# Block addresses, the order of loads at a stage turn, and the weight sums of the down projection in a one-core encoder layer

## The chip, the cores and the metric

The kernel runs on one core of a Trainium2 chip. The metric is the device time of one execution in microseconds (us). A core has a matrix engine (TensorE, PE in the profile, with PEld for its weight loads), a vector engine (VectorE, DVE), an activation engine (ScalarE, ACT), GpSimd (POOL), and SyncE (SP), which here issues nearly all DMA transfers. SBUF is the on-chip memory of 128 partitions, PSUM the accumulators that PE writes.

## The reference

One layer of a streaming encoder is applied to 512 prompt frames and 64 sample frames, all float32. The core of it is:

```python
hn = rmsnorm(x, g_norm1)
proj = hn @ w_in                                   # 2048 -> 6144
q, k, v, gb, gc, hc = split(proj)
o_attn = stick_breaking(q, k, v)                   # 8 heads x 128
o_conv = gb * conv3_causal(gc * hc)                # 1024 channels
x = x + concat(rmsnorm(o_attn), rmsnorm(o_conv)) @ w_out
h2 = rmsnorm(x, g_norm2)
x = x + (silu(h2 @ w_gate) * (h2 @ w_up)) @ w_down # 2048 -> 5632 -> 2048
```

The new keys, values and convolution state are outputs too.

## The kernel before, in words

The 576 frames are processed together, in two halves of 288 (`HALF`), so nearly every matmul has 288 moving columns of 128 partitions. Activations lie transposed: channels on partitions, frames along the free dimension. Float32 accuracy is reached by splitting each operand into a high part (rounded to float32r) and the rest: a product is three matmuls, high weight with high frames, low with high, high with low (`step`, `multiply`). The split is one ACT copy and one DVE subtraction (`split`, L211 and L212).

The kernel has five stages, in order of time. The start loads and transposes x. Then come the input projection with attention and convolution woven into it (`head`, `conv_group`, L203), the output projection (`out_proj`, L203), the gate and up projections, and the down projection. Gate, up and down use a one-level Strassen scheme of seven products (L1117): a unit is a block of a weight matrix, 256 rows times m pairs by 256 columns, and its products carry the numbers 1 to 7. Each product is m x 3 matmuls. Gate and up units have m = 8. `DOWN` lists the down units as (column block, first pair, last pair), so m is the difference; there are 8 column blocks and 22 pairs of hidden rows, each pair being seven operand forms in DRAM (`hid_dram`, 2,016 KB). Seven slots in SBUF hold pairs for the down stage; they lie in blocks that the gate and up stage uses until its last unit (`h2s`, `t12`, `t34`), so the pairs can only be loaded when the last products that read these blocks are done. This place is the turn.

Weights come from DRAM into two raw tiles, `raw_a` and `raw_b`, each with two halves of 2,048 values per partition. A down unit with m up to 4 takes one half (`room`), a larger one both halves of one tile. `prepare(n, p)` runs four products ahead (`AHEAD`): it forms the weight operand of product p of unit n and splits it into `whl`, of which there are four. Four sums of weight blocks are needed per unit (L1085 to L1087 and L1099, all DVE). In the gate and up units the first three stand ahead of product 6 and the last ahead of product 3. In the down units the first three stand together behind the operand of product 2. When both products 3 and 4 of a unit have been prepared, its raw halves are free and `load_columns` issues the next loads that find room.

`run(n, p)` issues the matmuls and what follows them: after products 1, 6 and 5 the partial sum in PSUM is copied out by ACT (`kept`, L1127), and later products go on adding into the same PSUM tile, so PE waits for that copy. DVE and POOL add the results into accumulators in SBUF. The last unit of a column block calls `store_y`: PE transposes the accumulator (L1268), DVE copies two 128x128 blocks out of PSUM (L1270), ACT the remaining 32 rows (L1272), and SP stores. `load_pair` issues the load of a pair, L1247 as one DMA or L1239 as seven.

Until the last gate and up unit the scheduler orders all engines but PE. From the first product of that unit on (`NGU - 1`), ACT, DVE, SP and POOL go in the order written. `turned` says behind which product of the last unit which pairs may be loaded, and `since` and `PACE` spread the loads.

Pools are placed one behind the other from both ends of SBUF. In the built program `h2_s` begins at byte 72,416, `xhi` and `t12` at 155,616, the first `x2` tile at 192,480 and `mixa_hi` at 118,048 of the partition: the remainders by 128 are 96, 96, 96 and 32. The raw and split weight tiles begin at multiples of 128. Every half of 288 float32 values is 1,152 bytes, nine times 128.

Of the kernel before, what the change touches and what calls it, by code (L numbers as in the profile page):

```python
# [34 lines left out]
NP = KD // 2  # L35
# [6 lines left out]


DOWN = (
# [5 lines left out]
)  # L50


# [41 lines left out]
def tile_hybrid_stream_step(  # L94
# [6 lines left out]
    nc = tc.nc  # L101
# [12 lines left out]
    wpool = ctx.enter_context(tc.tile_pool(name="wpool", bufs=2, side="left"))  # L114
    rpool = ctx.enter_context(tc.tile_pool(name="rpool", bufs=1, side="left"))
    tmp = ctx.enter_context(tc.tile_pool(name="tmp", bufs=2, side="left"))
    acon = tc.alloc_tile_pool(name="acon", bufs=1, side="left")
    xt_dram = tc.dram_tile([KD, P, T], F32, name="xt_dram")
    x2_dram = tc.dram_tile([KD, P, T], F32, name="x2_dram")
# [90 lines left out]
    def split(hi, lo, src, lo_eng=None):  # L210
        nc.scalar.copy(out=hi, in_=src)  # L211
        (lo_eng or nc.vector).tensor_tensor(out=lo, in0=src, in1=hi.bitcast(F32), op=ALU.subtract)  # L212
# [796 lines left out]

    def load_columns(gone=()):  # L1010

        free.extend(gone)
        while wanted and room(*wanted[0]):
            n, c = wanted.pop(0)
            kind, i, a, m = UNITS[n]
            w = {"gate": w_gate, "up": w_up, "down": w_down}[kind]
            halves = room(n, c)
            for h in halves:
                free.remove(h)
            t = raw_tile[halves[0][0]]  # L1020
            t = t[:, halves[0][1], :] if len(halves) == 1 else t.rearrange("p h e -> p (h e)")
            wide_ = P if c is not None else 2 * P
            c0 = 2 * i * P + (c or 0) * P
            t = t[:, : 2 * m * wide_]
            nc.sync.dma_start(out=t.rearrange("p (k e) -> p k e", e=wide_),
                              in_=w[2 * a * P : 2 * (a + m) * P, c0 : c0 + wide_].rearrange("(k p) c -> p k c", p=P))
# [50 lines left out]
    unit = {}  # L1077
    operand = {}
    slot_turn = [0]

    def weight_sums(n, st):
        m = UNITS[n][3]
        st["a21"], st["a22"] = (region[n, 1][0][:, :, q, :] for q in range(2))
        st["s1"] = w2pool.tile([P, NP, P], F32, tag="s1", name="s1")[:, :m]
        nc.vector.tensor_tensor(out=st["s1"], in0=st["a21"], in1=st["a22"], op=ALU.add)  # L1085
        nc.vector.tensor_tensor(out=st["a21"], in0=st["a21"], in1=st["a11"], op=ALU.subtract)
        nc.vector.tensor_tensor(out=st["a11"], in0=st["s1"], in1=st["a11"], op=ALU.subtract)  # L1087

    def prepare(n, p_):

        st = unit.setdefault(n, {})
        m = UNITS[n][3]
        if p_ == 1:
            st["a11"], st["a12"] = (region[n, 0][0][:, :, q, :] for q in range(2))
        src = {1: "a11", 2: "a12", 3: "a12", 4: "a22", 5: "s1", 6: "a11", 7: "a21"}[p_]
        if p_ == 6 and n < NGU:
            weight_sums(n, st)
        if p_ == 3:
            nc.vector.tensor_tensor(out=st["a12"], in0=st["a12"], in1=st["a11"], op=ALU.subtract)  # L1099
        slot_turn[0] += 1  # L1100
        whl = wpool.tile([P, 2, NP, P], F32R, tag=("whi", "wlo")[slot_turn[0] % 2], name="whl")[:, :, :m]
        split(whl[:, 0], whl[:, 1], st[src])
        operand[n, p_] = whl
        if p_ == 2 and n >= NGU:
            weight_sums(n, st)
        if p_ in (3, 4):
            st["gone"] = st.get("gone", 0) + 1
            if n < NGU:
                load_columns(region.pop((n, p_ - 3))[1])
            elif st["gone"] == 2:  # L1110
                load_columns(region.pop((n, 0))[1])

    def multiply(ps, n, p_, start):
        whl, xs_ = operand.pop((n, p_)), frames(n, p_)
# [78 lines left out]
    for d, v in visits.items():  # L1193
        n = next(a for a, b in zip(v, v[1:]) if a >= NGU + 10 and b >= a + 4)
# [54 lines left out]
    def store_y(n, c, i):  # L1249

        d = UNITS[n][1]
        src, cs, f0 = acc[d, c, i], slice((2 * d + c) * P, (2 * d + c + 1) * P), HALVES[i][0]
        r = HALF - 2 * P

        def put(f, ap):

            rows, n_p = ap.shape[0], max(min(TP - f, ap.shape[0]), 0)
            if n_p:
                nc.sync.dma_start(out=yp[f : f + n_p, cs], in_=ap[:n_p])  # L1259
            if n_p < rows:  # L1260
                nc.sync.dma_start(out=ys[f + n_p - TP : f + rows - TP, cs], in_=ap[n_p:])  # L1261

        def work():
            yield 9
            po = misc("pot")[:, : 3 * P]
            for q in range(3):
                w = min(P, HALF - q * P)
                nc.tensor.transpose(po[:w, q * P : (q + 1) * P], src[:, q * P : q * P + w], ident)  # L1268
            ob = src[:, : 2 * P].rearrange("p (i c) -> p i c", c=P)
            nc.vector.tensor_copy(out=ob, in_=po[:, : 2 * P].rearrange("p (i c) -> p i c", c=P))  # L1270
            obs = down["pool"].tile([r, P], F32, tag="obs", name="obs", bufs=2)
            nc.scalar.copy(out=obs, in_=po[:r, 2 * P :])  # L1272
            yield 5
# [14 lines left out]
    pairs = []  # L1288
    since = PACE
    mode = ExitStack()  # L1290
    AHEAD = 4
    for k_ in range(AHEAD):
        prepare(*order[k_])
    for k_, (n, p_) in enumerate(order):
        if (n, p_) == (NGU - 1, 1):
            mode.enter_context(tc.manual_schedule(engines={mybir.EngineType.Activation, mybir.EngineType.DVE,
                                                           mybir.EngineType.SP, mybir.EngineType.Pool}))
# [4 lines left out]
        pairs += turned.get((n, p_), calls[n - NGU] if n >= NGU and p_ == 4 else ())  # L1302
        since += UNITS[n][3]
        if pairs and since >= (PACE if n >= NGU else NP if pairs[0] < 2 else 2 * NP):
            load_pair(pairs.pop(0))
            since = 0
        if p_ == 2:
            for d in residual.get(n, ()):
                add_residual(d)
# [39 lines left out]
```

## Time and profile before

| | us |
|---|---|
| median of 3 runs | 2469.44 (2468.92 to 2475.55) |
| the profiled execution | 2472.84 |
| its span, first to last instruction | 2471.1 |
| PE busy | 2426.1 |
| DVE busy | 1746.7 |
| ACT busy | 1076.7 |
| POOL busy | 236.5 |

The profile is of one execution. The span is 1.7 us shorter than that execution's own time. An engine counts as busy while any of its instructions runs. Matmuls overlap: each lasts about 297 ns from its start to its modelled end, and the next begins long before. The rate of PE is therefore read from the starts or from the number of matmuls in a stretch, not from the duration of one.

### The profile page before, as it was taken

To read this page: it belongs to the slowest core of one execution; us is meant where nothing else is said; L and a number is where in the kernel's file an instruction comes from. 1 tells how busy PE (TensorE), PEld (TensorE's weight loads), DVE (VectorE), ACT (ScalarE), POOL (GpSimd) and SP (SyncE) were. 2 spreads that over 40 slices of the span, in tenths; PEclk is the share of its full clock that TensorE was granted. 3 is DMA by queue.
4 is the path that set the end of the run, shared out by engine and by line. 5 is a ranking of instruction groups with operands and counts; after the bars stand their busy time and mean duration, and the time that the engine had idled before them with its cause. 6 is when DMAs were issued, how large, how long until landed. Compare 5 with 4: busy or idle time off the path is not lost. (4 is left out here: it accounts for less than half of the span.)

```text
span 2471.1 us, 44086 instructions
## 1 busy us (share of the span) xinstructions
PE 2426.1 (98%) x18137; PEld 2412.7 (98%) x18137; DVE 1746.7 (71%) x2686; ACT 1076.7 (44%) x1907; POOL 236.5 (10%) x340
## 2 busy tenths in 40 slices
PE   8999999999999999999999999999999899999997
PEld 8999999999999999999999999999999899999996
DVE  7766666363335457888888888888887678877776
ACT  5655555231122345444444444444444344434433
POOL 2111010110020120000000000000000103321221
PEclk9999999999999999999999999999999999999999
DMA  8232322232243333535444455344445928874632
GB/s 269 79 96 87 87 79 84 71 99 76 81 149 99 105 129 115 153 114 151 146 142 129 138 151 155 117 149 144 146 138 160 314 73 244 235 208 140 207 120 69
DMA packets 464547, 336.50 MB, mean 136 GB/s; under 512 B 10207, under 2 KB 456537, under 8 KB 464345
## 3 DMA queue, kind: packets, MB, share of 16 engines
q1 hardware_dynamic: 459176, 326.90, 43.1%
q0 software_dynamic: 5168, 6.79, 1.5%
q8 instruction: 142, 2.33, 0.4%
q14 instruction: 61, 0.49, 0.1%
HBM read 269.33 MB, written 64.31 MB: 135 GB/s over the span
## 5 line engine op out<-in xcount | busy, mean ns | idle before, releaser
L1117 PE MATMUL psy<-t,whl 128*128 128x288 f32 x2916 | 443.2, 297 | 16.9 <-DMA t<-hid_dram 10.7
L203 PE MATMUL pj<-xhi,whi 128*128 128x288 f32 x1504 | 450.6, 300 | 0.0
L203 PE MATMUL pj<-xlo,whi 128*128 128x288 f32 x1504 | 444.7, 296 | 1.7 <-DVE xlo L337 1.7
L203 PE MATMUL pj<-xhi,wlo 128*128 128x288 f32 x1504 | 444.4, 295 | 0.3 <-DVE wlo L167 0.3
L1117 PEld LDWEIGHTS psy<-t,whl 128*128 128x128 f32 x2916 | 406.5, 190 | 20.5 <-DMA t<-hid_dram 10.9
L1117 PE MATMUL psy<-h_s,whl 128*128 128x288 f32 x2724 | 415.4, 297 | 8.3 <-ACT part L1127 7.6
L1117 PEld LDWEIGHTS psy<-h_s,whl 128*128 128x128 f32 x2724 | 380.7, 190 | 10.8 <-ACT part L1127 9.2
L1117 PE MATMUL psw<-t,whl 128*128 128x288 f32 x2592 | 379.3, 296 | 0.0
L1117 PEld LDWEIGHTS psw<-t,whl 128*128 128x128 f32 x2592 | 356.8, 189 | 0.1
L212 DVE TENSOR_TENSOR whl<-raw_a,whl 128x1024 fp32r<-128x1024 f32 (+5 forms) x276 | 297.6, 1079 | 69.1 <-ACT whl L211 68.6
L211 ACT CAST whl<-raw_a 128x1024 fp32r<-128x1024 f32 (+5 forms) x276 | 248.7, 909 | 126.7 <-DVE raw_a L1087 45.7
L203 PEld LDWEIGHTS pj<-xlo,whi 128*128 128x128 f32 x1504 | 284.1, 189 | 2.0 <-DVE xlo L337 2.0
L203 PEld LDWEIGHTS pj<-xhi,wlo 128*128 128x128 f32 x1504 | 284.4, 189 | 0.8 <-DVE wlo L167 0.5
L203 PEld LDWEIGHTS pj<-xhi,whi 128*128 128x128 f32 x1504 | 284.4, 189 | 0.4
L212 DVE TENSOR_TENSOR whl<-raw_b,whl 128x1024 fp32r<-128x1024 f32 (+5 forms) x204 | 203.2, 997 | 98.7 <-ACT whl L211 97.4
L211 ACT CAST whl<-raw_b 128x1024 fp32r<-128x1024 f32 (+5 forms) x204 | 168.8, 838 | 204.7 <-issue 73.8
L166 ACT CAST whi<-raw_a 128x1024 fp32r<-128x1024 f32 (+1 forms) x138 | 140.0, 1030 | 232.6 <-PE pj L203 95.8
L1127 ACT COPY part<-psy 128x288 f32<-128x288 f32 x240 | 95.5, 398 | 254.1 <-PE psy L1117 251.2
L167 DVE TENSOR_TENSOR wlo<-raw_a,whi 128x1024 fp32r<-128x1024 f32 (+1 forms) x132 | 160.3, 1227 | 23.8 <-ACT whi L166 22.5
L1117 PE MATMUL psx<-h_s,whl 128*128 128x288 f32 x1122 | 166.4, 297 | 0.0
L1117 PEld LDWEIGHTS psx<-h_s,whl 128*128 128x128 f32 x1122 | 155.7, 190 | 0.0
L211 ACT CAST whl<-s 128x1024 fp32r<-128x1024 f32 (+5 forms) x80 | 70.1, 876 | 70.0 <-PE psw L1117 68.5
(379 smaller groups left out, 3618.8 us busy)
## 6 DMA issues: line engine op xcount, KB each, us to landing
raw_a<-in_w_in_dram SPq DMA_DIRECT2D x47, 1024.0 KB, 5.5
hid_dram<-form SPq DMA_DIRECT2D x147, 288.0 KB, 2.4
raw_a<-in_w_gate_dram SPq DMA_DIRECT2D x23, 1024.0 KB, 5.4
raw_a<-in_w_up_dram SPq DMA_DIRECT2D x23, 1024.0 KB, 5.7
raw_b<-in_w_gate_dram SPq DMA_DIRECT2D x21, 1024.0 KB, 7.2
raw_b<-in_w_up_dram SPq DMA_DIRECT2D x21, 1024.0 KB, 6.9
h_s<-hid_dram SPq DMA_DIRECT2D x10, 2016.0 KB, 9.5
raw_a<-in_w_out_dram SPq DMA_DIRECT2D x16, 1024.0 KB, 5.3
```

What stands on the lines that cost most here:

```text
L166: nc.scalar.copy(out=hi[:, a:b], in_=raw[:, a:b])
L167: lo_eng.tensor_tensor(out=lo[:, a:b], in0=raw[:, a:b], in1=hi[:, a:b].bitcast(F32), op=ALU.subtract)
L203: mm(ps, w_[:, k, csl], x_[:, k, a:b], start=(k == 0 and n == 0), stop=(k == nk - 1 and n == 2))
L211: nc.scalar.copy(out=hi, in_=src)
L212: (lo_eng or nc.vector).tensor_tensor(out=lo, in0=src, in1=hi.bitcast(F32), op=ALU.subtract)
L1117: mm(ps, whl[:, w_, j, :], x_, start=(start and j == 0 and q == 0), stop=(j == len(xs_) - 1 and q == 2), skip_group_check=True)
L1127: nc.scalar.copy(out=t, in_=st["y"])
```

## The change

It has four parts.

- **Addresses.** Three unused tiles are allocated: 32 bytes on the left behind `tmp`, 224 bytes at the right end, 192 bytes in `cpool`. In the built program `h2_s` now begins at 72,448, `xhi` and `t12` at 155,392, the first `x2` tile at 192,256, `mixa_hi` at 118,272 and the attention tiles from 99,840 on, all multiples of 128. `tmp` and `rpool` stay where they were. Up to the turn, each engine's instructions are the same and in the same order as before.
- **The turn.** With the first product of the last gate and up unit, `hold` stops `load_columns`. `turned` now issues pairs 0 and 1, then pair 2 and one block of columns, then pair 3 and one block, then pairs 4 and 5; after the last product pair 6 is queued, `hold` ends and the remaining loads go out. `PACE` goes from 20 to 24. Before, blocks of columns for the second, third and fourth down units were issued between pairs 0, 1 and 2.
- **Down units and their weight sums.** `DOWN` is a new list of 37 units instead of 38; 16 have five pairs, and the last units of the column blocks have four to six instead of three to five. For a unit the four sums are made by a generator, one sum at a time: `prepare` of products 1, 6, 7, 5, 3 and 4 of the down units lets the oldest unit still summing make its next one, and `prepare` of 6 or 3 makes those that are still missing.
- **Output copies.** The copy of two 128x128 blocks in `store_y` goes from DVE to ACT, three steps behind the transposes instead of at once, and the stores four steps behind it instead of five.

```diff
+    lpad.tile([P, 8], F32, name="lpad_t")
+    rpad.tile([P, 56], F32, name="rpad_t")
...
+    cpool.tile([P, 48], F32, name="cpad_t")
...
-            return (lone or free)[:1]
+            return (lone or free)[-1:]
...
+    hold = []
+    def load_columns(gone=(), one=False):
         free.extend(gone)
-        while wanted and room(*wanted[0]):
+        while wanted and room(*wanted[0]) and (one or not hold):
             n, c = wanted.pop(0)
+            one = False
...
+    def weight_sums(n):
+        st, m, tt = unit[n], UNITS[n][3], nc.vector.tensor_tensor
...
+        tt(out=st["s1"], in0=st["a21"], in1=st["a22"], op=ALU.add)
+        yield
+        tt(out=st["a21"], in0=st["a21"], in1=st["a11"], op=ALU.subtract)
+        yield
+        tt(out=st["a11"], in0=st["s1"], in1=st["a11"], op=ALU.subtract)
+        yield 6
+        tt(out=st["a12"], in0=st["a12"], in1=st["a11"], op=ALU.subtract)
+        yield 3
...
         operand[n, p_] = whl
-        if p_ == 2 and n >= NGU:
-            weight_sums(n, st)
+        if n >= NGU:
+            if p_ == 1:
+                summing.append(n)
+            if summing and p_ != 2:
+                k = summing[0]
+                if unit[k]["summed"] != 6 or p_ == 6:
+                    one_sum(k)
+                if unit[k]["summed"] == 3:
+                    summing.pop(0)
...
-            nc.vector.tensor_copy(out=ob, in_=po[:, : 2 * P].rearrange("p (i c) -> p i c", c=P))
+            nc.scalar.copy(out=ob, in_=po[:, : 2 * P].rearrange("p (i c) -> p i c", c=P))
...
-    turned = {(NGU - 1, 2): (0, 1), (NGU - 1, 6): (2,), (NGU - 1, 7): (3,), (NGU - 1, 5): (4,),
-              (NGU - 1, 3): (5,), (NGU - 1, 4): (6,)}
-    PACE = 20
+    turned = {(NGU - 1, 2): (0, 1), (NGU - 1, 6): (2, "w"), (NGU - 1, 7): (3, "w"), (NGU - 1, 5): (4,), (NGU - 1, 3): (5,)}
+    PACE = 24
```

More of the change, by code (lines that the diff above doesn't have):

```diff
@@ L116, in tile_hybrid_stream_step @@
     tmp = ctx.enter_context(tc.tile_pool(name="tmp", bufs=2, side="left"))
+    lpad = ctx.enter_context(tc.tile_pool(name="lpad", bufs=1, side="left"))
+    lpad.tile([P, 8], F32, name="lpad_t")
+    rpad = ctx.enter_context(tc.tile_pool(name="rpad", bufs=1, side="right"))
+    rpad.tile([P, 56], F32, name="rpad_t")
     acon = tc.alloc_tile_pool(name="acon", bufs=1, side="left")
@@ L1079, in tile_hybrid_stream_step @@
     slot_turn = [0]
-    def weight_sums(n, st):
-        m = UNITS[n][3]
+    def weight_sums(n):
+        st, m, tt = unit[n], UNITS[n][3], nc.vector.tensor_tensor
         st["a21"], st["a22"] = (region[n, 1][0][:, :, q, :] for q in range(2))
         st["s1"] = w2pool.tile([P, NP, P], F32, tag="s1", name="s1")[:, :m]
-        nc.vector.tensor_tensor(out=st["s1"], in0=st["a21"], in1=st["a22"], op=ALU.add)
-        nc.vector.tensor_tensor(out=st["a21"], in0=st["a21"], in1=st["a11"], op=ALU.subtract)
-        nc.vector.tensor_tensor(out=st["a11"], in0=st["s1"], in1=st["a11"], op=ALU.subtract)
+        tt(out=st["s1"], in0=st["a21"], in1=st["a22"], op=ALU.add)
[6 more added lines that the diff above has]
+        yield 3
+    summing = []
     def prepare(n, p_):
-        st = unit.setdefault(n, {})
+        st = unit.setdefault(n, {"summed": -1})
         m = UNITS[n][3]
@@ L1094, in prepare @@
             st["a11"], st["a12"] = (region[n, 0][0][:, :, q, :] for q in range(2))
+        if p_ == 6:
+            while st["summed"] != 6:
+                one_sum(n)
+        if p_ == 3:
+            while st["summed"] != 3:
+                one_sum(n)
         src = {1: "a11", 2: "a12", 3: "a12", 4: "a22", 5: "s1", 6: "a11", 7: "a21"}[p_]
-        if p_ == 6 and n < NGU:
-            weight_sums(n, st)
-        if p_ == 3:
-            nc.vector.tensor_tensor(out=st["a12"], in0=st["a12"], in1=st["a11"], op=ALU.subtract)
         slot_turn[0] += 1
@@ L1103, in prepare @@
         operand[n, p_] = whl
-        if p_ == 2 and n >= NGU:
-            weight_sums(n, st)
+        if n >= NGU:
[7 more added lines that the diff above has]
+                    summing.pop(0)
         if p_ in (3, 4):
@@ L1111, in prepare, with one_sum @@
                 load_columns(region.pop((n, 0))[1])
+    def one_sum(n):
+        st = unit[n]
+        if "sums" not in st:
+            st["sums"] = weight_sums(n)
+        st["summed"] = next(st["sums"]) or 0
     def multiply(ps, n, p_, start):
@@ L1281, in store_y @@
         pipe.spawn(work())
-    turned = {(NGU - 1, 2): (0, 1), (NGU - 1, 6): (2,), (NGU - 1, 7): (3,), (NGU - 1, 5): (4,),
-              (NGU - 1, 3): (5,), (NGU - 1, 4): (6,)}
-    PACE = 20
+    turned = {(NGU - 1, 2): (0, 1), (NGU - 1, 6): (2, "w"), (NGU - 1, 7): (3, "w"), (NGU - 1, 5): (4,), (NGU - 1, 3): (5,)}
+    PACE = 24
     pairs = []
-    since = PACE
+    since = 0
     mode = ExitStack()
@@ L1295, in tile_hybrid_stream_step @@
         if (n, p_) == (NGU - 1, 1):
+            hold.append(True)
             mode.enter_context(tc.manual_schedule(engines={mybir.EngineType.Activation, mybir.EngineType.DVE,
@@ L1301, in tile_hybrid_stream_step @@
             prepare(*order[k_ + AHEAD])
[L1302 to L1306, printed above, removed]
+        for p in turned.get((n, p_), ()):
+            if p == "w":
+                load_columns(one=True)
+            else:
+                load_pair(p)
+        if (n, p_) == (NGU - 1, 4):
+            pairs.append(6)
+            since = -16
+            hold.clear()
+            load_columns()
+        if n >= NGU:
+            pairs += calls[n - NGU] if p_ == 4 else ()
+            since += UNITS[n][3]
+            if pairs and since >= PACE:
+                load_pair(pairs.pop(0))
+                since = 0
         if p_ == 2:
```

4 lines of the change are left out of this document (2 added, 2 removed), and 10 rows, old and new, of the table DOWN.

## The prediction, made before the changed kernel ran

> **What bounds the kernel now.** I read the page first (its first part), then the time by stages, then what PE waited for, and last the starts of single matmuls, because PE is busy nearly all the time and the question is how fast it runs while busy.
>
> ```profile
> span 2471.1 us, 44086 instructions
> ...
> PE 2426.1 (98%) x18137; PEld 2412.7 (98%) x18137; DVE 1746.7 (71%) x2686; ACT 1076.7 (44%) x1907; POOL 236.5 (10%) x340
> ```
>
> PE stands still for 45 us in all. No edit that only removes waits can gain more than that. The busy time by stages:
>
> ```profile
> 1050.00:1920.00 870.00, 870.00 (x6528) 870.00 (x6527) 721.42 (x986) 398.98 (x599) 1.70 (x2) 1.00 0.48 143
> 1920.00:1942.00 22.00, 11.34 (x72) 11.10 (x71) 11.40 (x25) 5.50 (x13) 3.64 (x5) 0.77 1.08 379
> 1942.00:2160.00 218.00, 214.26 (x1606) 212.60 (x1606) 171.52 (x248) 97.07 (x181) 49.90 (x55) 1.00 0.68 198
> 2160.00:2330.00 170.00, 170.00 (x1277) 170.00 (x1276) 126.53 (x160) 69.16 (x107) 33.42 (x37) 1.00 0.62 191
> 2330.00:2440.00 110.00, 102.24 (x741) 98.44 (x740) 84.34 (x144) 43.29 (x101) 23.61 (x24) 0.98 0.36 110
> 2440.00:2471.10 31.10, 19.82 (x145) 18.22 (x143) 16.28 (x34) 9.02 (x26) 5.21 (x6) 0.93 0.20 53
> ```
>
> Columns: stretch, its length, busy PE, PEld, DVE, ACT, POOL with instructions, granted PE clock, DMA share, GB/s. From 1050 to 1920 (gate and up) PE never stops: 6,528 matmuls in 870 us are 133.3 ns each, beside a DVE that is 83% busy. The turn lies in the second row: half its 22 us idle, the clock at 0.77, the DMA engines full (1.08). The down stage is idle for 3.7, 0, 7.8 and 11.3 us in the last four rows. What ended those waits:
>
> ```profile
> PE psy L1117 <- ACT part L1127: 12.2, 12, 2.4
> PE psy L1117 <- DMA t<-hid_dram: 10.7, 1, 10.7
> ...
> PE psy L1117 <- DVE whl L212: 2.6, 6, 0.8
> ```
>
> The 10.7 us is one wait, at the turn, for pair 2. The 12.2 us is PE waiting to add into a PSUM tile that ACT is still copying out.
>
> **The addresses.** This is the only part that touches the first 1,900 us, and no wait is in it; what it can change is the 133.3 ns. Two products of the input projection that differ only in the half of the frames:
>
> ```profile
> 503.11 0.30 PE L203 MATMUL pj<-xhi,whi 128*128 128x288 f32 x1
> ...
> 509.04 0.29 PE L447 MATMUL ssg<-sqg,oner 128*128 128x288 f32 x1
> ...
> 509.70 0.30 PE L203 MATMUL pj<-xhi,whi 128*128 128x288 f32 x1
> ...
> 516.10 0.30 PE L203 MATMUL pj<-xhi,whi 128*128 128x288 f32 x1
> ```
>
> From 503.11 to 509.04 are 45 matmuls of the second half: 131.8 ns each. From 509.70 to 516.10 are 48 of the first: 133.3 ns. By the allocation the first half starts at remainder 224 of 256, the second at 96, so the start address of the moving operand counts for 1.5 ns. No moving block of 288 columns lies at a multiple of 128 now; all will except those in `tmp`. A lower bound comes from the turn, where the clock was halved after the long wait:
>
> ```profile
> 1937.70 1.64 PE L1117 MATMUL psx<-h_s,whl 128*128 128x288 f32 x6
> 1939.14 0.92 PE L1117 MATMUL psx<-t,whl 128*128 128x288 f32 x3
> ```
>
> Six matmuls in 1.44 us are 240 ns, so 120 ns at full clock if the array itself sets the time. The 13.3 ns above that do not come from the array, since a halved clock would have doubled them too; they look like the supply of operands. Bounds for the new interval: 120 ns below, and 133.3 plus another 1.5 = 134.8 ns above, as the two address classes differ by that and the new ones (0 and 128 of 256) are in no row. I take a value near the rows that differ in nothing but the address, 131.8 to 133.3: 132.4 on average against 133.0 now (the mean of the two classes as they occur). Some 17,350 matmuls have 288 columns, so 0.6 ns is -10 us, with 0 to -21 us as this case's own ends.
>
> The Trainium skill, "SBUF — State Buffer", section "Door 1: The DMA port swizzle", says that SBUF has lines of 16 bytes and that a penalty comes from crossing into a new one; all blocks begin at multiples of 32 already, so by that the pads would gain 0, and the sum below would end at 2450 instead of 2440. The 1.5 ns above show that lines of 16 bytes are not the whole rule.
>
> **The turn.** SyncE's queue before:
>
> ```profile
> 1895.94 0.37 SPq L1025 DMA_DIRECT2D raw_a<-in_w_down_dram  x1
> 1901.03 0.36 SPq L1247 DMA_DIRECT2D h_s<-hid_dram  x1
> 1910.23 0.37 SPq L1025 DMA_DIRECT2D raw_b<-in_w_down_dram  x1
> 1910.69 2.25 SPq L1247 DMA_DIRECT2D h_s<-hid_dram  x1
> 1913.70 2.79 SPq L1025 DMA_DIRECT2D raw_a<-in_w_down_dram  x1
> 1916.58 3.10 SPq L1025 DMA_DIRECT2D raw_b<-in_w_down_dram  x1
> 1919.77 3.03 SPq L1247 DMA_DIRECT2D t<-hid_dram  x1
> 1922.89 13.74 SPq L1239 DMA_DIRECT2D t<-hid_dram  x7
> ```
>
> The queue stood at 1901 to 1910 behind a block of columns for which there was no room yet, then put pair 1, two more blocks (1 MB each) and only then pair 2. PE wants pair 2 at about 1926.2 and got it at 1936.8. After the change pairs 0 and 1 go at 1901 and pair 2 follows as soon as product 6 lets it: 3 x 2.06 MB at the 379 GB/s of the second stage row are 16.3 us, so pair 2 lands at 1917 to 1920. The wait goes, and with it the halved clock: 18 matmuls from 1936.8 to 1941.2 at 240 instead of 133 ns are 1.9 us. Together 12.6 us. Late next is the block of columns of the second unit, 1 MB behind pair 2 (3 us, so about 1923), whose ACT cast stands ahead of a copy that PE needs; then pair 3 and the 1.3 MB of the third unit, by 1932, wanted at about 1932 and 1938. That is narrow; I book -11, ends -12.6 and 0 (the DMA engines are full either way).
>
> **Weight sums and units.** Between product 1 and the next addition into its PSUM tile stands product 2, m x 3 matmuls: 1.2 us at m = 3, 2.0 us at m = 5. In that time ACT must finish its casts and the copy.
>
> ```profile
> L1127 ACT COPY part<-psy 128x288 f32<-128x288 f32 x110 | 43.6, 397 | 84.4 <-PE psy L1117 81.5 <-POOL acc L1149 2.0 <-DVE whl L212 0.9
> L1099 DVE TENSOR_TENSOR raw_b<-raw_b 128x640 f32<-128x640 f32 x6 | 6.1, 1017 | 0.0
> L1085 DVE TENSOR_TENSOR s<-raw_a 128x640 f32<-128x640 f32 x4 | 5.0, 1239 | 0.0
> ```
>
> Copy 0.4 us, one sum of five pairs 1.0 to 1.2 us. Three sums in one go hold DVE for 3.5 us and with it the low halves of the next operands; one at a time holds it for 1.2, beside a product of 2.0. Of the 3.7 us in 1942 to 2160 I book -2. In 2330 to 2440 five units of three pairs become longer ones: of its 7.8 us and 2% of clock (2 us) -5, and -3 of the last 11.3, most of which is the way of the last result out. Three units of three pairs remain, now at about 2300: +1. One unit fewer saves seven casts and four sums, all hidden beside PE. The ends: -14, and +5 if DVE's sums now stand ahead of evictions that PE waits for.
>
> **Output copies.**
>
> ```profile
> L1270 DVE COPY acc<-pot 128x256 f32<-128x256 f32 x20 | 8.1, 416 | 2.4 <-PE pot L1268 2.4
> L1272 ACT COPY obs<-pot 32x128 f32<-32x128 f32 x32 | 8.2, 255 | 53.3 <-issue 19.3 <-DVE acc L1270 13.6 <-DMA out_dram<-obs 10.2
> ```
>
> 32 copies of 0.42 us (13 us) leave DVE, where 84.34 of 110 us are used, for ACT with 43.29. Hidden but for the last one, which is now in a row with the 0.26 us copy: +0.3. If ACT were late, the 0.4 us would fall on PE's wait for `part`: +2 at most.
>
> **Sum.** -10 -11 -2 -5 -3 +1 +0.3 is -29.7, on the profiled execution's 2472.84: 2443.1. That execution is 3.4 above the median, 2469.44, to which the forecast is made: 2439.7, so 2440. Own range: -10 to -49, that is 2420 to 2459. Within 0.3% (7.4 us) this kernel can't be told from itself.
>
> **Rivals.**
> - *PE gets its operands at full rate.* If the 13.3 ns come from blocks that straddle 128 bytes, the interval falls toward the 120 ns of the halved clock. For: the excess is not the array's, and the address already moves it. Against: the best class so far saves only a tenth of it. At 123 ns, 17,350 x 10 ns = -174; turn and down -20; but DVE's 83% become 90%, so +10 of new waits: 2285, with 2262 to 2330 for 121 to 126 ns. The Trainium skill, "TensorE: Matmul & The Clock Gate", section "Back-to-back issue gap", gives N/2.4 + 2.5, 122.5 ns for 288 columns; that is an estimate by the page, and the trace's 133.3 does not agree with it.
> - *Columns arrive too late (slower).* With five pairs a unit takes both halves of a tile, so only two units are held. Columns are asked for when a unit's product 7 is done and needed five products of 15 matmuls later, 10 us, plus three prepared products, 6 us.
>
> ```profile
> raw_b<-in_w_down_dram SPq DMA_DIRECT2D x6, 1280.0 KB, 8.1
> ...
> t<-hid_dram SPq DMA_DIRECT2D x6, 2016.0 KB, 12.2
> ```
>
>   Behind a pair they need 12.2 + 8.1 = 20.3 us, 4.3 too many. With 15 pairs to load after the turn that is +64: 2440 + 64 = 2504. It decides from seven such units on (29.7 / 4.3). Against it: larger units did the same before, and 2160 to 2330 has no wait.
> - *The new addresses are the bad class.* +1.5 ns on 17,350 is +26 instead of -10: 2476. For: nothing is known of remainders 0 and 128, and the weights lie there too.
> - *Nothing happens.* Addresses 0, the turn bound by DMA anyway, sums hidden: 2462 to 2477, say 2467.
>
> **Chances.** Forecast 0.43, full rate 0.34, nothing 0.07, columns late 0.11, bad class 0.05. Faster by over 0.3% are the first two, 0.77; same 0.07; slower 0.16. The range 2262 to 2475 leaves out the late columns, most of the bad class and the lowest part of full rate, somewhat under 0.2.
>
> **What would show it.** Addresses: matmuls in 870 us of the gate and up stage, now 6,528; 6,570 is the forecast, 7,070 the full rate, 6,450 the bad class. Turn: no PE wait for `hid_dram`, and the clock at 1.00. Sums: PE's wait on `part` under 7 us. Columns late: ACT's casts waiting for `raw_a` or `raw_b` from DMA. I would be wrong above all if the excess of 13.3 ns is one of alignment altogether, or not at all.

## The result and the profile after

Measured beside each other, the kernel before takes 2472.49 us (median) and the changed one 2435.21 us (2433.88 to 2435.53). The ratio is 0.9845, 95% interval 0.9828 to 0.9862: 1.5% faster. Measured again later it was 2435.42 against 2475.84, ratio 0.9845 (0.983 to 0.9859). The forecast was 2440, with 2420 to 2459 as its own range. The profiled executions stand at 2472.84 and 2433.88, 39.0 us apart.

The page of the changed kernel, first part:

```profile
span 2432.2 us, 44020 instructions
...
PE 2406.1 (99%) x18137; PEld 2397.9 (99%) x18137; DVE 1739.8 (72%) x2639; ACT 1085.1 (45%) x1929; POOL 231.3 (10%) x337
```

PE has as many instructions as before and is 20 us less busy. So part of the gain is a shorter interval between matmuls, and the rest, 19 us of the span's 39, is idle time. Its time by stages (length, busy PE, PEld, DVE, ACT, POOL with instructions, granted clock, DMA share, GB/s):

```profile
1050.00:1900.00 850.00, 850.00 (x6430) 850.00 (x6430) 712.41 (x974) 395.02 (x594) 0.95 (x1) 1.00 0.45 142
1900.00:1930.00 30.00, 23.69 (x169) 23.45 (x168) 21.43 (x40) 10.45 (x23) 4.38 (x6) 0.89 1.08 393
1930.00:2130.00 200.00, 199.93 (x1512) 199.69 (x1511) 160.16 (x220) 90.98 (x162) 38.58 (x44) 1.00 0.63 191
2130.00:2300.00 170.00, 170.00 (x1288) 170.00 (x1287) 138.10 (x188) 73.24 (x126) 43.87 (x48) 1.00 0.69 216
2300.00:2400.00 100.00, 99.72 (x762) 99.22 (x761) 75.87 (x102) 49.15 (x112) 19.98 (x21) 1.00 0.40 122
2400.00:2432.20 32.20, 24.95 (x189) 24.05 (x187) 14.82 (x23) 12.38 (x35) 4.82 (x6) 0.95 0.18 49
```

6,430 matmuls in 850 us are 132.2 ns each; 133.3 before. The down stage has 0.1, 0, 0.3 and 7.3 us of idle PE where it had 3.7, 0, 7.8 and 11.3. The turn is the row that has not come clean: 6.3 us idle, and the clock at 0.89. PE's waits in the changed kernel (us in total, times, longest):

```profile
PE psy L1150 <- ACT part L1160: 8.4, 3, 6.3
PE psx_s L321 <- DMA xsn<-in_x_sample_dram: 4.7, 2, 4.5
PE pj L208 <- DVE xlo L342: 2.2, 1, 2.2
```

The wait for pair 2 is gone, and so are most of the waits for `part`, which had been twelve. One is new, 6.3 us long, at the turn:

```profile
1916.67 0.95 PE L1150 MATMUL psx<-h_s,whl 128*128 128x288 f32 x6
...
1918.07 0.56 DVE L1099 TENSOR_TENSOR raw_a<-s,raw_a 128x384 f32<-128x384 f32 x1
1918.74 0.51 ACT L216 CAST whl<-raw_a 128x384 fp32r<-128x384 f32 x1 [1.66 <-DVE raw_a L1099]
...
1921.20 0.46 DVE L978 TENSOR_TENSOR ux<-ux,gs 128x288 f32<-128x288 f32 x1
1921.69 0.43 ACT L216 CAST form<-ux 128x288 fp32r<-128x288 f32 x1 [2.45 <-DVE ux L978]
...
1923.14 0.43 ACT L216 CAST acc_z<-ux 128x288 fp32r<-128x288 f32 x1 [1.02 <-DVE ux L944]
1923.48 0.51 ACT L216 CAST whl<-raw_a 128x384 fp32r<-128x384 f32 x1
1923.89 0.39 ACT L1160 COPY part<-psy 128x288 f32<-128x288 f32 x1
...
1924.34 1.09 PE L1150 MATMUL psy<-h_s,whl 128*128 128x288 f32 x3 [6.31 <-ACT part L1160]
```

This is the changed kernel's timeline (start, duration, engine, line; idle time before and its releaser in brackets). Unit 0's product 1 was ending when product 2 (`psx`) began at 1916.67, but its copy comes at 1923.89: it stands on ACT behind four casts, three of which wait for a DVE that is working off the evictions of the last gate and up unit and unit 0's sums one after the other.

To book the 39 us, take each matmul's interval from start to start and subtract a fixed one for its shape (133.3 ns for 288 columns); sums by stretch of the two profiled executions, in us:

| Stretch | before | after | difference |
|---|---|---|---|
| up to 1050 | 10.8 | 8.5 | -2.3 |
| 1050 to 1900, gate and up | 0.2 | -6.9 | -7.1 |
| the turn, 1900 to 1960 | 12.6 | 7.6 | -5.0 |
| 1960 to 2330 | 4.4 | -1.9 | -6.3 |
| from 2330 | 19.4 | 1.1 | -18.3 |

### The profile page after: what moved, and what is told of

It is laid out like the page before. It is cut to its first block, busy times and chain, and to the rows that moved or that the text cites. A ratio compares the mean times of both kernels' runs of the same rounds, so it can differ in the third digit from the quotient of the medians.

```text
span 2432.2 us, 44020 instructions
## 1 busy us (share of the span) xinstructions
PE 2406.1 (99%) x18137; PEld 2397.9 (99%) x18137; DVE 1739.8 (72%) x2639; ACT 1085.1 (45%) x1929; POOL 231.3 (10%) x337
## 4 chain that ended last, share of the span: by engine, by line
PE 94%; DVE 3%; DMA 1%; ACT 1%; issue 0%; SPq 0%; ACTq 0%; DVEq 0%
PE psy L1150 32%; PE pj L208 24%; PE psw L1150 16%; PE pjo L208 8%; PE psx L1150 8%; PE pw L993 2%; DVE xlo L342 1%; PE z L547 1%; PE po L613 1%; DVE whl L217 1%; PE pot L1301 0%; DMA raw_a<-in_w_down_dram 0%; PE os L643 0%; PE zs L573 0%; PE pjz L208 0%
## 5 line engine op out<-in xcount | busy, mean ns | idle before, releaser
L217 DVE TENSOR_TENSOR whl<-raw_a,whl 128x1024 fp32r<-128x1024 f32 (+4 forms) x288 | 312.9, 1087 | 59.7 <-ACT whl L216 58.5
L216 ACT CAST whl<-raw_a 128x1024 fp32r<-128x1024 f32 (+4 forms) x288 | 259.4, 902 | 112.0 <-issue 35.4
L217 DVE TENSOR_TENSOR whl<-raw_b,whl 128x1024 fp32r<-128x1024 f32 (+5 forms) x186 | 197.1, 1060 | 69.2 <-ACT whl L216 68.3
L216 ACT CAST whl<-raw_b 128x1024 fp32r<-128x1024 f32 (+5 forms) x186 | 161.0, 868 | 161.3 <-issue 69.6
```

## The experiments

Times are medians; "beside" is the kernel before in the same session.

**Each part alone.** Theory after the result: the four parts add up, the address part -10, the turn -5, the rest in the down stage.

```diff
 # pads_only: the kernel before, and
+    lpad.tile([P, 8], F32, name="lpad_t")
+    rpad.tile([P, 56], F32, name="rpad_t")
+    cpool.tile([P, 48], F32, name="cpad_t")
```

> The kernel before with the three pads alone; order of work, units and copies as before. Theory: the start address of the moving operand is a cause by itself, so the mean interval of the 288-column matmuls falls from 133.0 to about 132.4 ns, 6,581 matmuls per 870 us in the gate and up stage, and the time falls by 10 us (8 to 13), to about 2462. Rival A: the faster interval of the changed kernel comes from its other order of work, and the stage stays at 6,528 per 870 us: 0 us. Rival B: alignment frees the port altogether only together with something else: also 0 here. PE's waits at the turn and after it stay as they were.

Measured 2462.81 beside 2475.16, ratio 0.9952 (0.9937 to 0.9967): -12.4. The profiled executions differ by 11.3; by the booking 2.5 of it fall before 1050, 7.1 in the gate and up stage, and 1.9 at the turn, where no wait was expected to change.

```diff
 # schedule_only: the changed kernel, and
-    lpad.tile([P, 8], F32, name="lpad_t")
-    rpad.tile([P, 56], F32, name="rpad_t")
-    cpool.tile([P, 48], F32, name="cpad_t")
```

> The changed kernel without the three pads: new order of loads, new units, spread sums, output copies on ScalarE, old addresses. Theory: it loses only the address term, so 2435 + 10 = 2445 (2443 to 2449), with 6,528 matmuls per 870 us in the gate and up stage, and the down stage as free of waits as in the changed kernel. Rival: the slower interval of before hides evictions, and with it back the down stage has still fewer waits: 2440 or less.

Measured 2445.95 (2439.3 to 2447.28), ratio 0.9885 (0.9869 to 0.9902). The time is as expected, but the profiled execution, the one of 2439.3, did not show the 6,528. Here are two stretches in which PE never waits, of the kernel before:

```profile
1100.00:1900.00 800.00, 800.00 (x6003) 800.00 (x6002) 668.33 (x914) 369.08 (x555) 0.00 (x0) 1.00 0.47 140
2200.00:2300.00 100.00, 100.00 (x752) 100.00 (x751) 72.11 (x91) 40.78 (x60) 15.97 (x18) 1.00 0.54 172
```

of `schedule_only`, with the same addresses:

```profile
1100.00:1900.00 800.00, 800.00 (x6052) 800.00 (x6052) 672.11 (x920) 371.23 (x558) 0.95 (x1) 1.00 0.48 142
2200.00:2300.00 100.00, 100.00 (x752) 100.00 (x751) 78.58 (x115) 42.75 (x77) 20.68 (x23) 1.00 0.63 203
```

and of `pads_only`:

```profile
1100.00:1900.00 800.00, 800.00 (x6053) 800.00 (x6052) 671.13 (x919) 373.48 (x559) 0.95 (x1) 1.00 0.46 143
2200.00:2300.00 100.00, 100.00 (x758) 100.00 (x758) 72.02 (x91) 41.27 (x62) 17.05 (x19) 1.00 0.53 174
```

There are two steady rates, 6,000 or 6,050 matmuls in 800 us (the counts hold up to three that reach over an edge), that is 133.33 or 132.22 ns. With the old addresses a stage runs at either: `schedule_only` has the fast one up to 1900 and the slow one at 2200, and `turn_only`, below, the other way round (6,002 and 759). In the gate and up stage, where PE never stops, each trace keeps its rate throughout. In the down stage the rate can change: the kernel before has 607 matmuls from 1960 to 2040 and 602 from 2170 to 2250, and `units_only`, below, 607 from 2000 to 2080 but 603 from 2110 to 2190, with a wait of 5.7 us between the two. With the pads of the change, all eight profiled executions had the fast one in both stretches above. So the pads do not make a matmul faster than it could be before; as far as these executions show, they take away the slow rate. Over the 850 us of gate and up the difference is 7.1 us, and three of the four times of `schedule_only` lie 5.5 to 8 above the profiled one; that those three had the slow rate there is not shown.

Besides the moving blocks the pads move the raw tile `raw_b`, which in the kernel before begins at byte 130,016, with a remainder of 96 and not at a multiple of 128; PE doesn't read it. The split weights `whl`, which PE reads, lie at the same bytes in both kernels.

```diff
 # turn_only: the kernel before, and
-            return (lone or free)[:1]
+            return (lone or free)[-1:]
-        while wanted and room(*wanted[0]):
+        while wanted and room(*wanted[0]) and (one or not hold):
...
+    turned = {(NGU - 1, 2): (0, 1), (NGU - 1, 6): (2, "w"), (NGU - 1, 7): (3, "w"), (NGU - 1, 5): (4,), (NGU - 1, 3): (5,)}
+    PACE = 24
```

> The kernel before with the new order of loads at the turn alone (held blocks, pair 2 with no block ahead of it, pace 24), with the old units, whose sums come in one go, and the old addresses. Theory: the wait of 10.7 us for pair 2 goes, and in its place PE waits about 6 us for ScalarE's copy of unit 0's first product, which stands behind the evictions of the last gate and up unit; -5 us, about 2467. Rival A, the prediction's term: -11 us, about 2461, no such wait with the old units. Rival B: with three sums in one go the copy is later still, the wait is 9 us or more, and the edit gains nothing: 2470 to 2475.

Measured 2467.53 (2459.82 to 2470.42), ratio 0.9962 (0.9951 to 0.9974): -7.6 by medians and -5.9 between the profiled executions, nearer the theory than rival A. PE's first row of waits:

```profile
PE psy L1120 <- ACT part L1130: 15.8, 12, 4.9
```

The wait for pair 2 is gone, and one of 4.9 us for `part` stands there, with the old units as well. Here unit 0's sums stand ahead of these evictions on DVE; in the changed kernel they stand among them, and the wait is 6.3. By the booking above the turn costs 6.6 us (12.6 before). Rival B falls; the prediction's full -11 does too.

```diff
 # units_only: the kernel before, with DOWN, weight_sums, prepare and one_sum of the changed kernel
```

> The kernel before with the new list of units and the spread sums alone; the turn, the addresses and the output copies as before. Theory: the down stage loses nearly all of its waits (before 3.7, 0, 7.8 and 11.3 us idle in its four stretches, in the changed kernel 0.1, 0, 0.3 and 7.3), so -15 to -18 us, about 2456, while the wait of 10.7 us for pair 2 stays. Rival, the prediction's terms: -2 -5 -3 +1 = -9 us, about 2463; then the rest of the gain in the down stage belongs to the order of loads.

Measured 2459.33 (2452.73 to 2462.7), ratio 0.9934 (0.9917 to 0.9952): -15.8 by medians; the profiled execution is the slowest of the four and only 10.1 under that of before. By the medians the theory's size holds, but its account of the waits does not. PE from 1915 on:

```profile
PE psy L1141 <- ACT part L1151: 13.8, 7, 5.7
PE psy L1141 <- DMA t<-hid_dram: 1.9, 1, 1.9
```

The wait of 10.7 us for pair 2, which was to stay, is one of 1.9: SyncE issues the pair at 1914.65, right behind pair 1, and not at 1919.77 behind two blocks. At 1936.80 PE has waited 3.9 us for `part` instead. By the booking the turn costs 9.0 us (12.6 before), so part of this run's gain lies there. And further on a block of columns came late. ACT of this kernel:

```profile
2099.79 0.72 ACT L211 CAST whl<-raw_b 128x640 fp32r<-128x640 f32 x1 [9.76 <-DMA raw_b<-in_w_down_dram]
2100.43 0.39 ACT L1151 COPY part<-psy 128x288 f32<-128x288 f32 x1
```

and PE:

```profile
2100.87 0.61 PE L1141 MATMUL psy<-h_s,whl 128*128 128x288 f32 x1 [5.71 <-ACT part L1151]
```

with SyncE's queue ahead of it:

```profile
2074.77 4.83 SPq L1263 DMA_DIRECT2D t<-hid_dram  x7
2080.44 0.36 SPq L1271 DMA_DIRECT2D t<-hid_dram  x1
2085.13 2.73 SPq L1025 DMA_DIRECT2D raw_b<-in_w_down_dram  x1
```

The block was issued 5 to 10 us behind the eight transfers of two pairs, and the copy of `part` stood behind its cast. That is the prediction's rival of late columns, once, for 5.7 us instead of 4.3; in the changed kernel, with its other order at the turn and its other pace of pairs, it does not occur; which of the two keeps it out was not separated. By the booking this execution gains 9.4 us from 1960 on, or 15.1 without the late block.

```diff
 # sums_only: the kernel before, with weight_sums, prepare and one_sum of the changed kernel
```

> The kernel before with the spread weight sums alone; old list of units, old turn, old addresses, old output copies. Theory: the waits of the down stage come from units of three pairs, whose product 2 is too short for ScalarE's copy, and not from the three sums in one go; so the waits after 2330 us stay (19 us above the ideal interval before), and the gain is 1 to 4 us: 2471 to 2474. Rival, as the prediction booked part of it: sums in one go hold VectorE and with it the low halves; then 8 us or more go, about 2466.

Measured 2471.61 (2461.84 to 2474.12) beside 2475.63, ratio 0.9985 (0.9971 to 1.0): -4.0. Its waits are those of before in number:

```profile
PE psy L1141 <- ACT part L1151: 13.8, 12, 2.3
```

Spreading the sums alone leaves twelve waits for `part`. With the longer units beside it, in `units_only`, five short ones are left behind the late block, 4.2 us in all, and in the changed kernel one of 0.5 us behind the turn. The longer units without the spread sums were not run.

**The output copies.**

```diff
 # copies_dve: the changed kernel, and
-            yield 3
             ob = src[:, : 2 * P].rearrange("p (i c) -> p i c", c=P)
-            nc.scalar.copy(out=ob, in_=po[:, : 2 * P].rearrange("p (i c) -> p i c", c=P))
+            nc.vector.tensor_copy(out=ob, in_=po[:, : 2 * P].rearrange("p (i c) -> p i c", c=P))
...
-            yield 4
+            yield 5
```

> The changed kernel with the 32 large output copies back on VectorE and their old delays. Theory: they are hidden on either engine, 0 to +1 us, 2434 to 2437. Rival: in the last 30 us they stand ahead of evictions on VectorE that PE waits for, and give back 2 to 4 us: 2437 to 2440.

Measured 2441.34 (2440.7 to 2443.69), ratio 0.9876 (0.9853 to 0.99): 6 us slower than the changed kernel, more than the rival. The copies in `copies_dve`, from 1895 on (count, busy us, mean ns, then idle time before and what ended it):

```profile
L1303 DVE COPY acc<-pot 128x256 f32<-128x256 f32 x20 | 8.2, 417 | 1.2 <-PE pot L1301 1.2
L1305 ACT COPY obs<-pot 32x128 f32<-32x128 f32 x32 | 8.2, 256 | 66.0 <-issue 20.5 <-DVE acc L1303 19.9 <-DMA out_dram<-obs 10.7
```

and in the changed kernel:

```profile
L1306 ACT COPY obs<-pot 32x128 f32<-32x128 f32 x32 | 8.0, 251 | 9.6 <-DMA out_dram<-obs 9.6
L1304 ACT COPY acc<-pot 128x256 f32<-128x256 f32 x20 | 7.4, 368 | 3.7 <-PE pot L1301 3.7
```

With the large copy on DVE, ACT's small copy out of the same PSUM tile waits for it, 19.9 us where the large copy goes to `acc` and 34.7 with the other three accumulators, and the copies of `part` stand behind it on ACT: PE waits for them 3.4 us in five times behind the turn, 0.5 in the changed kernel. With both on ACT that wait is gone. It is a wait for a semaphore of DVE's, so the built program sets this order; no run shows what the chip does without it. The large copy also takes 368 instead of 417 ns on ACT. The edit takes away the three steps between the transposes and the copies as well, so how much of the 6 us belongs to the engine and how much to the delay is not separated.

**What the addresses do.**

```diff
 # pads_64: pads_only, and
-    lpad.tile([P, 8], F32, name="lpad_t")
-    rpad.tile([P, 56], F32, name="rpad_t")
+    lpad.tile([P, 24], F32, name="lpad_t")
+    rpad.tile([P, 40], F32, name="rpad_t")
```

> The kernel before with pads of other sizes, so that the blocks begin at odd multiples of 64 bytes (64 and 192 of 256) instead of 0 and 128; nothing else. In the traces so far the stage of the gate and up units runs at one of two steady rates, 133.33 or 132.22 ns per matmul; with the old addresses both occur, with the pads only the faster one was seen. Theory A: what matters is 128 bytes, the unit in which operands are fetched; then this kernel behaves as the one before, mostly 133.33 ns, 2469 to 2477. Theory B: what matters is 64 bytes (the old blocks begin 32 beside a multiple of 64); then it behaves as with the pads of the change, 2461 to 2465.

Measured 2474.75 (2472.79 to 2478.46), ratio 1.0005 (0.9993 to 1.0016): nothing is gained, as by theory A, and its profiled execution has the slow rate in both stretches (6,002 and 753). So moving the blocks is not enough; of the three sets of addresses only the one at multiples of 128 gains. That operands are fetched in units of 128 bytes is shown by no run.

```diff
 # streams: the changed kernel, and behind its end
+    def stream(offsets, cols, count=48):
+        for s in offsets:
+            ps = ps_pj.tile([P, HALF], F32, tag="pj", name="pps")
+            seq = s if isinstance(s, tuple) else (s,)
+            for i in range(count):
+                o = seq[i % len(seq)] // 4
+                mm(ps[:, :cols], pw[:, (i % 16) * P : (i % 16 + 1) * P], pm[:, o : o + cols],
+                   start=(i == 0), stop=(i == count - 1))
```

> The changed kernel with streams of matmuls behind its end, with nothing else on the chip's engines: 48 matmuls of 288 columns each from start addresses 0, 32, 64, ... 224 of 256 bytes, then 192 matmuls of triples as the units have them (two from one block, one from the next, 1152 bytes on) from 0, 128, 64, 192, 96 and 224, then 256 columns from 0, 96 and 224. Its total time says nothing of the change. Theory A: the excess over 120 ns and its dependence on the address belong to the supply of operands of one matmul: every stream keeps its own interval, 131 to 134 ns, least at the addresses at which a block touches fewest lines of 128 or 256 bytes. Theory B: the excess comes from other engines at the same memory; then the streams here run at 120 to 125 ns at every address. For triples, the slower steady rate of 133.33 ns is expected from 96, 224, 64 and 192, and 132.22 from 0 and 128.

PE's timeline inside streams from 0, 32, 128 and 4 bytes, then of triples from 0, 96 and 224 (`pm` begins at a multiple of 256):

```profile
2450.81 5.69 PE L1382 MATMUL pps<-pm,pw 128*128 128x288 f32 x42
...
2457.13 5.77 PE L1382 MATMUL pps<-pm,pw 128*128 128x288 f32 x42
...
2476.05 5.90 PE L1382 MATMUL pps<-pm,pw 128*128 128x288 f32 x43
...
2514.41 5.86 PE L1382 MATMUL pps<-pm,pw 128*128 128x288 f32 x42
...
2520.78 24.92 PE L1382 MATMUL pps<-pm,pw 128*128 128x288 f32 x187
...
2622.78 25.09 PE L1382 MATMUL pps<-pm,pw 128*128 128x288 f32 x187
2648.38 24.96 PE L1382 MATMUL pps<-pm,pw 128*128 128x288 f32 x186
```

and the same trace by windows (columns as above), no engine but PE and PEld being busy:

```profile
2440.00:2700.00 260.00, 260.00 (x1976) 260.00 (x1975) 0.00 (x0) 0.00 (x0) 0.00 (x0) 1.00 0.00 1
```

A row of the timeline is (count - 1) intervals and one last matmul of about 0.295 us. With all starts of each stream the mean intervals are:

| Start, bytes of 256 | 0 | 16 | 32 | 64 | 96 | 128 | 160, 192, 224 | 4 |
|---|---|---|---|---|---|---|---|---|
| ns per matmul, 288 columns | 131.7 | 131.5 | 133.3 | 131.7 | 131.7 | 133.4 | 133.2 to 133.3 | 135.6 |

Triples take 132.4 and 132.2 from 0 and 128, 133.3 from 64, 96 and 224, and 132.6 from 192. So theory B falls: with the other engines idle the excess over 120 ns is still there, the address alone moves the interval by 1.6 ns, and the kernel's two rates come back. Whether the excess is the moving operand's or that of the weight load beside each matmul, the streams can't tell: PEld is busy in them all the time. All expected triples but that from 192 are met. Not met is the guess that the number of lines touched decides: a block from 0 and one from 128 touch as many lines of 128 bytes (9), and as many of 256 (5). What the rule is stays open.

**The new wait at the turn.** Theory: the in-order evictions on ACT and DVE. The first edit moves one eviction.

```diff
 # late_forms: the changed kernel, and
-            st["p1"] = kept("ms")
+            st["p1"] = kept("t" if n == NGU else "ms")
+            while late:
+                late.pop(0)()
...
+            if n == NGU - 1:
+                spare_tile("z", 2)
+                late.append(lambda: done(1, 0, st["w"], st["u2"]))
```

> The changed kernel, with the evictions of the last product of the last gate and up unit issued behind the copy of unit 0's first product instead of ahead of it (the copy into another tile, so that it need not wait for them). Theory: the 6.3 us wait of the changed kernel at the turn comes from that copy standing on ScalarE behind casts that wait for VectorE; it falls under 1.5 us, the halved clock goes with it, and the time falls by 4 to 6 us, to about 2430. Rival A: pair 2 or the columns of the second unit land only just then; the wait stays at 4 us or more under another name, and the time at 2433 to 2436. Rival B: the delayed forms hold back the accumulators that ScalarE and VectorE need next: slower, 2438 or more.

Measured 2435.44 (2434.06 to 2435.64), ratio 0.9849 (0.983 to 0.9868): no gain. PE at the turn:

```profile
1922.14 1.06 PE L1150 MATMUL psy<-h_s,whl 128*128 128x288 f32 x6 [1.99 <-ACT part L1162]
...
1928.11 1.60 PE L1150 MATMUL psy<-h_s,whl 128*128 128x288 f32 x6 [3.32 <-ACT part L1162]
```

The 6.3 us became two waits, of 2.0 and 3.3, both on `part` and neither on a transfer: rival A falls in its reason, though its time is the one measured. The second copy now stood behind two casts of the delayed evictions, which waited 2.2 and 1.0 us for DVE, and then needed a tile that DVE gave back behind the same evictions, as ACT's row has it:

```profile
1927.65 0.40 ACT L1162 COPY part<-psy 128x288 f32<-128x288 f32 x1 [0.55 <-DVE acc_z L1177]
```

```diff
 # turn_reordered: the changed kernel, and
+            st["p1"] = kept("t" if n == NGU else "ms")
...
+                late[NGU, 5] = lambda: done(1, 0, st["w"], st["u2"])
...
+                late[n, 3] = lambda: done(0, 1, st["y"])
...
+            if order[k_ + AHEAD] == (NGU, 2):
+                while unit[NGU]["summed"] != 6:
+                    one_sum(NGU)
+        if (n, p_) in late:
+            late.pop((n, p_))()
```

> The changed kernel with its turn reordered on ScalarE and VectorE: unit 0's three sums before the evictions of the last gate and up unit, the evictions of its product 3 behind the next operand's cast, and those of its product 4 behind unit 0's product 5. Theory: the time PE loses at the turn (7.6 us in the changed kernel, 7.0 in two pieces when one copy alone was moved) is the in-order queue of evictions on ScalarE and VectorE, not data that lands late; then most of it goes, the two waits together are under 2 us and the time is 2429 to 2431. Rival: the columns of the second unit or pair 2 land no earlier than about 1923 us; then PE waits there for an operand instead, and the time stays at 2433 to 2436.

Measured 2432.7 (2431.51 to 2434.89), ratio 0.9836 (0.9809 to 0.9863). The turn costs 4.6 us by the booking, against 7.6 in the changed kernel; the theory's direction holds, its size does not. PE's wait at the turn:

```profile
1921.66 1.81 PE L1150 MATMUL psy<-h_s,whl 128*128 128x288 f32 x6 [2.26 <-ACT part L1162]
```

Besides the evictions, unit 0's three sums have moved: they now stand ahead of them. In the last edit, which keeps that, the evictions come form by form, each behind a product's copy and cast.

```diff
 # turn_pieces: turn_reordered with finish and put_forms as generators, a yield after each form, and
+    when = {(NGU - 1, 3): 2, (NGU, 1): 1, (NGU, 7): 1, (NGU, 5): 9}
...
+        for _ in range(when.get((n, p_), 0)):
+            while late and next(late[0], late) is late:
+                late.pop(0)
```

> The changed kernel with the reordered turn, and the evictions of the last gate and up unit cut into pieces: two forms behind product 3, one behind unit 0's product 1, one behind its product 7, the last behind its product 5, each behind the copy and the operand cast of that product. Theory: ScalarE's copy then waits for PE alone, the wait at the turn (7.6 us in the changed kernel, 4.6 in the reordered one) falls under 1.5 us and the clock stays at 1.00: 2427 to 2429, and 4 to 7 us under the changed kernel measured beside it. Rival: five pieces put a wait of 1 us each in the queue ahead of the later copies, and the loss stays at 4 us or more: 2431 to 2433.

> The changed kernel itself, beside the kernel with its turn in pieces: 2433 to 2437.

Measured 2431.84 (2430.34 to 2435.03, five runs), ratio 0.9831 (0.9815 to 0.9846), and beside it the changed kernel 2435.42 (2435.27 to 2436.88, four runs). That is 3.6 us less, with no run in common, and less than the theory's 4 to 7. PE at the turn:

```profile
1920.55 1.09 PE L1158 MATMUL psy<-h_s,whl 128*128 128x288 f32 x6 [0.47 <-ACT part L1171]
...
1924.23 1.06 PE L1158 MATMUL psy<-h_s,whl 128*128 128x288 f32 x6 [1.00 <-ACT part L1171]
...
1929.18 1.06 PE L1158 MATMUL psy<-h_s,whl 128*128 128x288 f32 x6 [1.91 <-ACT part L1171]
```

Three short waits are left of the long one, all for `part`, and the granted clock is 1.00 from 1916 to 1935. By the booking 3.8 us are still lost at the turn, where the changed kernel, profiled again beside it, loses 8.2, so the rival's size was nearly right as well. The last two edits change nothing but the order of work on ACT and DVE and the tile of one copy, the loss falls with both, and no transfer ended any of these waits: so this order is the cause of the new wait. How much of it belongs to the evictions and how much to unit 0's sums was not separated, and how low the loss can go was not found.

## Why the prediction was right, point by point

- *Addresses, -10: right in size, half right in its reason.* The interval was put at 133.0 now and 132.4 after; over all matmuls of 288 columns it came out at 132.98 and 132.37 in the profiled executions. By time the pads alone are worth 12.4. The start address does count for 1.5 ns, and the streams show it by itself. But the new addresses are again one good and one bad class (131.7 at 0, 133.4 at 128), as the old ones were; what is gained is that the triples no longer settle at the bad one's interval. The 132.4 was a choice between the two classes, for addresses that were in no row; that it came out to a tenth is luck. The forecast of 6,570 matmuls in 870 us came out at 6,430 x 870 / 850 = 6,581.
- *The lower bound of 120 ns* was rightly doubted. In the halved clock after the turn's wait (granted 0.50 from 1937.7 to 1939.8 before), matmuls still stand 240 ns apart, while no stream of 288 columns at full clock, with the other engines idle, goes under 131.5. The rival of full rate (0.34) falls: the excess belongs to the stream itself, and alignment moves a tenth of it. The bad class and "nothing happens" fall with the measured time.
- *The Trainium skill's 16-byte lines*, "SBUF — State Buffer", section "Door 1: The DMA port swizzle", would have the pads gain 0. The stream that starts 4 bytes into such a line does take 3.9 ns more (135.6 against 131.7 at 0 and 131.5 at 16), in the rule's direction; the 12 us between two sets of addresses that are both multiples of 32 are outside it.
- *The turn, -11: the step that failed.* Pair 2 came in time and its wait went, as put. "Late next" named the columns and ACT's casts ahead of a copy that PE needs. The copy was right and the columns were wrong: the casts ahead of it wait for unit 0's sums and for the evictions of the last gate and up unit, and these evictions had been late in the kernel before as well, under the wait for pair 2. Its DVE, with the last eviction:

```profile
1931.90 0.46 DVE L212 TENSOR_TENSOR acc_z<-ux,acc_z 128x288 fp32r<-128x288 f32 x1 [0.50 <-ACT acc_z L211]
```

  PE's wait for the pair ended at 1936.8. Booked -11, measured -5.0 in the profile. The sign named for it was missed, as the clock at the turn is 0.89 and not 1.00, and the one named for the sums was missed through it: PE waits 8.4 us on `part` and not under 7, 6.3 of them here.
- *Weight sums and units, -9: too small.* From 1960 on the profile gives -24.6. Of this about 2 us are the rate, as the kernel before left the fast one only at about 2150, and 6 the copies, so about -17 are left; `units_only` has -15.1 there without its late block. The term was sized as a half or two thirds of the waits of before. In the changed kernel nearly all of them are gone: PE waits 0.5 us for `part` behind the turn, 10.9 before. The +1 for the remaining units of three pairs was too careful; that stretch now waits 0.3 us.
- *Output copies, +0.3: wrong in sign, -6.* Their cost on ACT was counted, and what they would no longer hold up was not, though the row of `obs` quoted beside it said "DVE acc L1270 13.6".
- *Late columns (0.11)* is a real mechanism: it came up in `units_only`. In the changed kernel it doesn't occur; the prediction had not weighed what the new order and pace of the pairs do to it.

The four errors of size, -2, +6, -8 and -6, cancel in part, and that the time came within 5 us of the forecast owes something to it: the sum was -29.7, against -39.0 in the profile. Taken singly by medians the parts give -12.4 -7.6 -15.8 -6.1 = -41.9 (the copies as 2435.21 less 2441.34), against -37.3 and -40.4 for the whole in two sessions. That this comes near is itself a sum of opposites: by the booking the turn's gain of 5.0 us stands in it once as 6.0, in `turn_only`, and again as 3.6, in `units_only`, while `units_only` also pays 5.7 for the late block, which the whole does not have.

## What to carry to other kernels

When a wait goes, look through the queues of the waiting engine's helpers for what had been just as late under its cover; here half of the turn's gain went to evictions that had ended 4.5 us before the old wait did. When an instruction moves to another engine, count not only its duration but the waits that others had on it, in the rows of its neighbours. And when a stream of equal matmuls keeps one interval to the nanosecond for hundreds of microseconds, that interval can be one of two states, and start addresses can decide whether the slower one occurs: it is worth a test with a pad.

## What was not expected of the hardware

- A stream of 288-column float32r matmuls has two steady rates, 133.33 and 132.22 ns, with the same code and addresses, and keeps one of them for hundreds of microseconds; behind a wait the other was seen (607 matmuls in 80 us ahead of the 5.7 us in `units_only`, 603 behind it). What decides which one it takes was not found.
- The interval depends on the start of the moving block within 256 bytes: 131.5 to 131.7 ns from 0, 16, 64 and 96, 133.2 to 133.4 from 32, 128, 160, 192 and 224, and 135.6 from 4. In the streams of 256 columns a matmul takes 119.9 ns from 0 and from 96 and 118.3 from 224, so the order is not the same there.
